# A short load ahead of the first load of a 2x2x2 average pooling

## The chip, the cores and the metric

The kernel runs on one core of one Trainium2 chip. The metric is the device time of one execution in microseconds (us), the median over several runs.

## What is computed

The input `x` is a float32 tensor of 8 x 32 x 32 x 32 x 32 (batch, channels, depth, height, width), 33.55 MB. Each output element is the mean of a block of 2 x 2 x 2 inputs, so the output is 8 x 32 x 16 x 16 x 16 float32, 4.19 MB.

```python
for i in range(out_d):
    for j in range(out_h):
        for k in range(out_w):
            window = x[:, :, 2*i:2*i+2, 2*j:2*j+2, 2*k:2*k+2]
            result[:, :, i, j, k] = np.mean(window, axis=(-3, -2, -1))
```

## The kernel before

Batch and channel together are 256 rows of 32768 floats. They are taken as two halves `t` of 128 rows, one row for each partition. Along a row the work is cut at multiples of `KF` = 256 floats. The list `plan` (L42) has eight entries: four for each half, each with 32 x 256 floats per partition, which is a tile of 128 rows with 32 KB, 4 MB in all. The first six entries are loaded by one DMA each; the last two are cut into two loads of 2 MB each. That makes ten loads, all issued from SP's queue at L77. The tiles `tin` come from a pool of five buffers (`pool_in`, L36), so the first five loads need no free buffer, and each later one waits until VectorE has finished with the buffer five tiles before.

For each loaded part, `pool_unit` (L53) runs three instructions on VectorE: an addition of neighbouring depth planes (L58), an addition of neighbouring columns (L62), and an addition of neighbouring lines with the factor 0.125 (L65), which writes into `obuf`, one buffer for each half. The result is written out by four stores (L92): one of 256 KB from ACT's queue, and on SP's queue, in this order, 2 MB (the whole first half), 1.5 MB and 256 KB.

The order of SP's queue is thus: the ten loads, then three stores. Each load or store counts up one of eight semaphores when it has landed; they are given out in turn, and a semaphore comes round again after eight transfers. A transfer that takes one up again waits until the one before on it has landed.

After tracing, `tile_avg_pool_3d_kernel` edits the program by hand. The first load, `tin` of the first entry, is moved into the opening block, ahead of SP's `Drain`, the instruction with which SP enters the barrier of all engines that opens the program:

```python
    barrier = next(
        n for n, i in enumerate(opening)
        if i.engine == load.engine and isinstance(i, mybir.InstDrain))
    program.remove(load)
    opening.insert(barrier, load)
```

So it is the first thing that SP does; the second load is issued after the barrier. The same function rewrites the end: the semaphores of the four stores (`kept`) are waited for and reset by SP's last instructions, and the others are cleared by GpSimd in ranges that leave out those of the stores.

Of the kernel before, what the change touches and what calls it, by code (L numbers as in the profile page):

```python
# [1 line left out]

# [4 lines left out]

F32 = mybir.dt.float32
KF = 256


@with_exitstack
def pool_rows(
    ctx: ExitStack,
    tc: tile.TileContext,
    x: bass.AP,
    kernel_size: int,
    out: bass.AP,
):
    nc = tc.nc  # L20
    assert kernel_size == 2, "only kernel_size == 2 supported"

    B, C, D, H, W = x.shape
    P = nc.NUM_PARTITIONS
    assert (B * C, D, H, W) == (2 * P, 32, 32, 32)
    add = mybir.AluOpType.add

    xv = x.rearrange("b c d h w -> (b c) (d h w)")  # L30
    ov = out.rearrange("b c d h w -> (b c) (d h w)")

    pool_in = ctx.enter_context(tc.tile_pool(name="pin", bufs=5))  # L36
    pool_out = ctx.enter_context(tc.tile_pool(name="pout", bufs=1))
    obuf = [pool_out.tile([P, 16 * KF], F32, name=f"obuf{t}") for t in range(2)]
    dummy = pool_out.tile([P, 1], F32, name="dummy")


    plan = [  # L42
        (0, 0, (32,)),
        (0, 32, (32,)),
        (0, 64, (32,)),
        (0, 96, (32,)),
        (1, 0, (32,)),
        (1, 32, (32,)),
        (1, 64, (16, 16)),
        (1, 96, (16, 16)),  # L50
    ]

    def pool_unit(buf, t, k0, kb):  # L53

        od = kb // 8
        a = buf.rearrange("p (o dd e) -> p o dd e", o=od, dd=2)
        b = buf[:, :od * 1024]
        nc.vector.tensor_add(  # L58
            out=b.rearrange("p (o e) -> p o e", o=od), in0=a[:, :, 0], in1=a[:, :, 1])
        bv = b.rearrange("p (e ww) -> p e ww", ww=2)  # L60
        c = buf[:, od * 1024:od * 1536]
        nc.vector.tensor_add(out=c, in0=bv[:, :, 0], in1=bv[:, :, 1])  # L62
        cv = c.rearrange("p (j hh k) -> p j hh k", hh=2, k=16)
        o0 = k0 * KF // 8
        nc.vector.tensor_tensor_reduce(  # L65
            out=obuf[t][:, o0:o0 + od * 256].rearrange("p (j k) -> p j k", k=16),
            in0=cv[:, :, 0], in1=cv[:, :, 1],
            scale=0.125, scalar=0.0, op0=add, op1=add, accum_out=dummy[:, :],
        )

    for t, k0, parts in plan:
        tin = pool_in.tile([P, 32 * KF], F32, tag="tin", name="tin")
        views = []
        o = 0
        for kb in parts:
            v = tin[:, o * KF:(o + kb) * KF]
            nc.sync.dma_start(  # L77
                out=v, in_=xv[t * P:(t + 1) * P, (k0 + o) * KF:(k0 + o + kb) * KF])
            views.append((v, k0 + o, kb))
            o += kb  # L80
        for v, k, kb in views:
            pool_unit(v, t, k, kb)

    for queue, t, k0, kb in [
        (nc.scalar, 1, 0, 2),
        (nc.sync, 0, 0, 16),
        (nc.sync, 1, 2, 12),
        (nc.sync, 1, 14, 2),  # L90
    ]:
        queue.dma_start(  # L92
            out=ov[t * P:(t + 1) * P, k0 * KF:(k0 + kb) * KF],
            in_=obuf[t][:, k0 * KF:(k0 + kb) * KF],
        )


def kernel(tc: tile.TileContext, x: bass.AP, kernel_size: int, out: bass.AP):
    nc = tc.nc
    pool_rows(tc, x, kernel_size, out)  # L100
    tc.close()
    tc.compile()  # L102
    blocks = nc.main_func.blocks

    opening, program = blocks[0].instructions, blocks[tc.starting_block_idx].instructions
    load = next(i for i in program if isinstance(i, mybir.InstDMACopy))
    assert load.engine == nc.sync.engine
    barrier = next(  # L110
        n for n, i in enumerate(opening)
        if i.engine == load.engine and isinstance(i, mybir.InstDrain))
    program.remove(load)
    opening.insert(barrier, load)

    closing = blocks[-1].instructions
    stores = [  # L120
        i for i in program
        if isinstance(i, mybir.InstDMACopy) and "out_" in i.outs[0].memref]
    kept = [u.id for i in stores for u in i.sync_info.on_update]
    kept = [n for j, n in enumerate(kept) if n not in kept[j + 1:]]
    final = next(
        i for i in closing
        if i.engine == nc.sync.engine and isinstance(i, mybir.InstDrain))
    waits = {w.id: w for w in final.sync_info.on_wait}
    closing[closing.index(final)] = mybir.InstDrain(
        name=final.name, engine=final.engine, ins=[], outs=[], is_reset_sema=False,  # L130
        sync_info=mybir.SyncInfo(
            on_wait=[w for n, w in waits.items() if n not in kept], on_update=[]))


    reset = next(
        n for n, i in enumerate(closing)
        if isinstance(i, mybir.InstDrain) and i.is_reset_sema)
    first, stop = closing[reset].reset_range_start, closing[reset].reset_range_stop
    assert isinstance(closing[reset + 1], mybir.InstISA)
    while len(closing) > reset:  # L140
        closing.pop()
    n = first
    while n < stop:
        m = n
        while m < stop and m not in kept:
            m += 1
        if m > n:
            closing.append(mybir.InstDrain(
                name=nc.get_next_instruction_name(), engine=nc.gpsimd.engine, ins=[], outs=[],
                is_reset_sema=True, reset_range_start=n, reset_range_stop=m))  # L150
            nc.gpsimd.sem_clear(range(n, m))
        n = m + 1
    for n in kept:
        w = waits[n]
        closing.append(mybir.InstEventSemaphore(
            name=nc.get_next_instruction_name(), engine=nc.sync.engine, ins=[], outs=[],
            sync_info=mybir.SyncInfo(
                on_wait=[w],
                on_update=[mybir.SyncUpdate(
                    sync_type="semaphore", id=n, ant_name=w.ant_name,  # L160
                    update_mode="sem-sub-imm", update_value=w.wait_value)])))


# [1 line left out]
_INS = ['x', 'kernel_size']  # L165
_OUTS = [((8, 32, 16, 16, 16), 'float32')]

_NUMBERS = {'kernel_size': 2}


# [26 lines left out]
```

## Time and profile before

| what | value |
|---|---|
| median of 3 runs | 91.57 us (91.52 to 91.82) |
| the profiled execution, device time | 91.76 us |
| its span, first to last instruction | 86.6 us |
| VectorE busy | 64.1 us, 74% of the span |
| mean of the DMA engines' rate over the span | 421 GB/s |
| HBM read, written | 33.55 MB, 4.19 MB |

The span ends with the last instruction that the page counts, and the last stores land after it; the device time covers them too. The DMA rows of the page give the share of the 16 DMA engines that is busy and what they moved. A packet is booked by its start and its length, so in very short windows a share can be over 1. Some packet records are missing: the page counts 36.48 MB where the kernel moves 37.75 MB. A name ending in q, as in SPq, is the engine's instruction queue: SPq at L77 is SP issuing a load, and "to landing" is the time from the issue to the completed transfer.

### The profile page before, as it was taken

To read this page: it belongs to the slowest core of one execution; us is meant where nothing else is said; L and a number is where in the kernel's file an instruction comes from. 1 tells how busy PE (TensorE), PEld (TensorE's weight loads), DVE (VectorE), ACT (ScalarE), POOL (GpSimd) and SP (SyncE) were. 2 spreads that over 40 slices of the span, in tenths; PEclk is the share of its full clock that TensorE was granted. 3 is DMA by queue.
4 is the path that set the end of the run, shared out by engine and by line. 5 is a ranking of instruction groups with operands and counts; after the bars stand their busy time and mean duration, and the time that the engine had idled before them with its cause. 6 is when DMAs were issued, how large, how long until landed. Compare 5 with 4: busy or idle time off the path is not lost.

```text
span 86.6 us, 91 instructions
## 1 busy us (share of the span) xinstructions
DVE 64.1 (74%) x40; POOL 0.2 (0%) x4
## 2 busy tenths in 40 slices
DVE  0000049993999749992999749992999999999994
POOL 0000000000000000000000000000000000000000
DMA  8889998899979999799988999699999999999999
GB/s 242 379 363 469 485 485 348 379 485 485 469 333 409 485 485 424 318 469 485 485 348 379 485 485 469 288 454 416 405 407 424 407 462 394 462 394 454 394 454 398
DMA packets 1774, 36.48 MB, mean 421 GB/s; under 512 B 192, under 2 KB 192, under 8 KB 320
## 3 DMA queue, kind: packets, MB, share of 16 engines
q1 hardware_dynamic: 1630, 36.22, 98.4%
q10 hardware_dynamic: 144, 0.26, 0.8%
HBM read 33.55 MB, written 4.19 MB: 436 GB/s over the span
## 4 chain that ended last, share of the span: by engine, by line
DMA 83%; DVE 14%; SPq 1%; issue 0%; DVEq 0%
DMA tin<-in_x_dram 83%; DVE tin L58 8%; DVE tin L62 4%; DVE obuf L65 2%; SPq L77 1%; DVE dummy L65 0%; DVEq L102 0%
## 5 line engine op out<-in xcount | busy, mean ns | idle before, releaser
L58 DVE TENSOR_TENSOR tin<-tin 128x4096 f32<-128x4096 f32 (+1 forms) x10 | 35.7, 3570 | 20.7 <-DMA tin<-in_x_dram 20.6
L62 DVE TENSOR_TENSOR tin<-tin 128x2048 f32<-128x2048 f32 (+1 forms) x10 | 18.6, 1865 | 0.3
L65 DVE CUSTOM_DVE_ANT_1 obuf<-tin 128x1024 f32<-128x1024 f32 (+1 forms) x10 | 10.1, 1011 | 0.3
L65 DVE DVE_READ_ACCUMULATOR2_ANT dummy<- 128x1 f32 x10 | 0.8, 82 | 0.0
L178 POOL MEMSET const-uint8-127<- 128x1 uint8 x1 | 0.1, 102 | 0.0
L178 POOL MEMSET const-bfloat16-1.0<- 128x1 bf16 x1 | 0.1, 101 | 0.0
L178 POOL MEMSET const-float32-0.0<- 128x1 f32 x1 | 0.1, 98 | 0.2 <-issue 0.2
L178 POOL MEMSET const-float32-1.0<- 128x1 f32 x1 | 0.1, 98 | 0.0
## 6 DMA issues: line engine op xcount, KB each, us to landing
tin<-in_x_dram SPq DMA_DIRECT2D x6, 4096.0 KB, 35.0
tin<-in_x_dram SPq DMA_DIRECT2D x4, 2048.0 KB, 38.9
out_dram<-obuf SPq DMA_DIRECT2D x1, 2048.0 KB, 36.8
out_dram<-obuf SPq DMA_DIRECT2D x1, 1536.0 KB, 8.8
out_dram<-obuf ACTq DMA_DIRECT2D x1, 256.0 KB, 9.9
out_dram<-obuf SPq DMA_DIRECT2D x1, 256.0 KB, 4.9
```

What stands on the lines that cost most here:

```text
L58: nc.vector.tensor_add(out=b.rearrange("p (o e) -> p o e", o=od), in0=a[:, :, 0], in1=a[:, :, 1])
L62: nc.vector.tensor_add(out=c, in0=bv[:, :, 0], in1=bv[:, :, 1])
L65: nc.vector.tensor_tensor_reduce(out=obuf[t][:, o0:o0 + od * 256].rearrange("p (j k) -> p j k", k=16), in0=cv[:, :, 0], in1=cv[:, :, 1], s ...
L77: nc.sync.dma_start(out=v, in_=xv[t * P:(t + 1) * P, (k0 + o) * KF:(k0 + o + kb) * KF])
L178: nc = _bacc.Bacc("TRN2", target_bir_lowering=False, num_devices=1)
```

## The change

A tile `first` of 16 partitions x 128 floats is added to the pool of output buffers, and a load of the first 512 B of 16 rows of `x` into it, 8 KB in all, is traced ahead of everything else. Nothing reads this tile. The hand edit then moves two loads instead of one ahead of SP's `Drain` in the opening block: the short one, and behind it the first load of `tin`.

```diff
     dummy = pool_out.tile([P, 1], F32, name="dummy")
+    first = pool_out.tile([16, 128], F32, name="first")
+    nc.sync.dma_start(out=first[:, :], in_=xv[:16, :128])
...
-    load = next(i for i in program if isinstance(i, mybir.InstDMACopy))
-    assert load.engine == nc.sync.engine
-    barrier = next(
-        n for n, i in enumerate(opening)
-        if i.engine == load.engine and isinstance(i, mybir.InstDrain))
-    program.remove(load)
-    opening.insert(barrier, load)
+    loads = [i for i in program if isinstance(i, mybir.InstDMACopy)][:2]
+    assert [i.outs[0].bass_ap.tensor.name.split("_")[0] for i in loads] == ["first", "tin"]
+    for load in loads:
+        assert not load.sync_info.on_wait
+        barrier = next(
+            n for n, i in enumerate(opening)
+            if i.engine == load.engine and isinstance(i, mybir.InstDrain))
+        program.remove(load)
+        opening.insert(barrier, load)
```

## The prediction

> **What bounds the kernel now.** I read the page first, its section 2 and 4: how full the DMA engines are over time, and what the chain that ended last is made of.
>
> ```profile
> DVE  0000049993999749992999749992999999999994
> ...
> DMA  8889998899979999799988999699999999999999
> ...
> DMA 83%; DVE 14%; SPq 1%; issue 0%; DVEq 0%
> ```
>
> The reader is to see that the DMA row never drops, from the second slice to the last, while VectorE (DVE) has holes up to the last third. Next come the stores, by their line in the two windows in which they are issued: is the end set by the last store's own latency, or by what lies ahead of it?
>
> ```profile
> L92 SPq DMA_DIRECT2D out_dram<-obuf x1: 348/348/348, 49.3 to 49.3; - x1
> DMA to landing us min/median/max: 9.9/23.3/36.8
> ...
> L92 SPq DMA_DIRECT2D out_dram<-obuf x2: 332/338/344, 81.1 to 85.5; - x2
> DMA to landing us min/median/max: 4.9/6.8/8.8
> ```
>
> The 2 MB store is issued at 49.3 and lands 36.8 later, at 86.1. The 1.5 MB store, issued at 81.1, lands 8.8 later, at 89.9; the last, of 256 KB, issued at 85.5, lands 4.9 later, at 90.4. So after the last load (landed by 81.2, when VectorE starts on it) the engines still have a full queue: 2 + 1.5 + 0.25 MB, 3.93 MB in 9.2 us, 427 GB/s. The loads run at the same pace: VectorE starts on the first three tiles at 12.12, 21.81 and 31.53, 9.7 us apart, 4.19 MB / 9.7 = 432 GB/s. **The kernel is one unbroken stream of transfers**, and its end is the start of that stream plus 37.75 MB of work. VectorE is done at 85.46, and the 256 KB that wait for it could come 3 us later, with about 1 us from issue to first packet (below) still inside the 4.4 us until 89.9. So a shift of the stream's start moves the end by as much, and little else does.
>
> How does the stream start? L77 in the first tenth of a us, the opening barrier's line, and the DMA share in windows of 0.1 us (the columns after the window: length, DVE and POOL busy, PEclk, share of 16 DMA engines, GB/s):
>
> ```profile
> L77 SPq DMA_DIRECT2D tin<-in_x_dram x1: 382/382/382, 0.0 to 0.0; - x1
> ...
> L178 SPq DRAIN  x1: 132/132/132, 0.4 to 0.4; - x1
> ...
> 0.90:1.00 0.10, 0.00 (x0) 0.00 (x0) 1.00 0.00 0
> 1.00:1.10 0.10, 0.00 (x0) 0.00 (x0) 1.00 6.01 1638
> 1.10:1.20 0.10, 0.00 (x0) 0.00 (x0) 1.00 4.80 1311
> 1.20:1.30 0.10, 0.00 (x0) 0.00 (x0) 1.00 2.23 655
> 1.30:1.40 0.10, 0.00 (x0) 0.00 (x0) 1.00 2.16 655
> 1.40:1.50 0.10, 0.00 (x0) 0.00 (x0) 1.00 0.00 0
> 1.50:1.60 0.10, 0.00 (x0) 0.00 (x0) 1.00 0.98 328
> 1.60:1.70 0.10, 0.00 (x0) 0.00 (x0) 1.00 0.00 0
> 1.70:1.80 0.10, 0.00 (x0) 0.00 (x0) 1.00 1.82 655
> 1.80:1.90 0.10, 0.00 (x0) 0.00 (x0) 1.00 0.00 0
> ...
> 2.80:2.90 0.10, 0.00 (x0) 0.00 (x0) 1.00 1.54 655
> ...
> 5.10:5.30 0.20, 0.00 (x0) 0.00 (x0) 1.00 0.38 164
> ```
>
> The first load is issued at 0.00 in 0.38 us. Sixteen packets of 32 KB (GB/s x 0.1 us, summed over these windows to 1.80: 524 KB) begin between 1.00 and 1.80. Their length is share x 16 x window: 18.0 x 1.6 = 28.8 engine-us, 1.80 each; the first five 6.01 x 1.6 / 5 = 1.92, the last two 1.82 x 1.6 / 2 = 1.46. Later packets take 0.38 x 16 x 0.2 = 1.22. The first packets are thus **0.58 us longer** on average than a packet in full flow. The second packets begin from 2.80 on.
>
> **What the Trainium skill says.** "DMA: Bandwidth & Descriptors", "Latency and other measured facts", gives some 600 ns to the first byte for DMAs from SP. The trace agrees: from the issue's end at 0.38 to the first packets at 1.00 is 0.62. The same page, "Why a DMA increments its semaphore by 16 and not by 1", spreads a transfer of 16 rows over 16 engines: one row of 512 B on each, so the short load stands ahead of the first load everywhere. The trace of before has no transfer of 16 rows. The same page, "Queues, rings and completion order", has descriptors of a ring taken in order, with no barrier between data descriptors. The trace fits: 9.7 us per load over 8 rows per engine is 1.21 per row across the load's end, no more than inside a load.
>
> **The change, part by part.**
>
> Added issue: one DMA on SP, ahead of the first load. The shape seems to make little difference: issues take 0.33 to 0.53 at L77, the first 0.38, the second 0.33. The first load of `tin` is handed over after two issues: 0.38 + (0.33 to 0.38) instead of 0.38. **Cost on the path: 0.33 to 0.38, taken as 0.36.** Nothing covers it, since no transfer is in flight.
>
> Added transfer: 512 B per engine, at 32 KB in 1.22 us, 0.02 us. Its own latency runs in the time in which the next issue is made; no instruction reads `first`. Taken as 0.02; bounds 0 and, if the packet holds its engine until it is complete, see rival B.
>
> The barrier: SP's Drain comes at about 0.75 instead of 0.4 and holds all engines, so the second load is issued at about 1.15 instead of 0.79, and loads 3 to 5 behind it. Cover: each engine has eight packets of the first load to do, until about 11.4; counting 1 us to the first packet, the second load could be issued 9 us later. VectorE has nothing to do before 12, ACT before its store at 59.0, and GpSimd's memsets are over by 0.43.
>
> Semaphores: the load takes the first of eight, all others move by one. By the code each store still finds itself behind the load that it was behind before (tiles 3 to 5); the seventh tile's load meets the short load's semaphore, complete some 30 us earlier: one check, 17 ns as SP's others, in a queue 30 us ahead. At the end the stores' semaphores lie at the range's end, so GpSimd may have one range to clear instead of two: that lies around 86.2 to 86.6, beside stores in flight to 90.4. Nothing; without that cover, a gain of some tenths. `first` takes 512 B per partition behind the other buffers and moves none.
>
> What the first packets lose or gain is not shown before. **Below nothing:** if the 0.58 is the cost of waking engines and memory, the short packets pay it from 1.00 on, while the second issue runs, and up to 0.58 comes back. **Above nothing:** the engines could start on the long row only when the short one is complete. I take 0: a packet that must wait for its first data has the same length behind a short one, and that need not be a matter of waking.
>
> Sum: 0.36 + 0.02 = 0.38. The profiled execution, with span 86.6, lasts 91.76, of which 1.4 follow the last landing at 90.4: 92.14 on its own terms. It lies 0.19 above the median of the runs shown, inside their spread, so the forecast is 91.57 + 0.38 = **91.95 us**, 0.4% slower. A measurement of this kernel can tell about 0.3% from no change, 0.27 us, so this lies just past the bound.
>
> **The rivals.**
>
> A, not slower: **the short load wakes the engines.** For it: early starters need 1.92 and late ones 1.46, which end at about 2.95 and 3.2, as if something common were ready only at about 1.7, whoever asked first. Against it: that is also what filling a pipeline looks like, and the wake-up can begin no earlier than now, since the first issue is still at 0.00. Price: 0.38 less what is saved. From 0.11 saved on the change is inside the 0.3%; all 0.58 saved gives 91.57 - 0.20 = 91.37, still no measurable gain. Faster by over 0.27 needs 0.65 saved, so also a part of the 0.62 from issue to first packet: with the issue shift half hidden too (0.18), 91.19.
>
> B, much slower: **the short transfer is completed first.** The skill's same page, "Anatomy of one DMA — SWDGE (gpsimd) path", prices a transfer's fixed part at some 2.0 us, mostly completion; for this queue that is an estimate. If the long row begins only then, at 2.0 instead of 1.0, the cost is 1.0: 92.57. Against it: at the ends of loads nothing of the kind shows.
>
> C: the shift is taken up along the way. The stream has dips, the lowest slice 288 GB/s, but records are missing, and no wait of the queue for a buffer empties it: four loads stand behind. Then 91.6.
>
> **How the numbers follow.** Forecast 0.55, of which 0.06 falls inside the bound; A 0.32, of which 0.15 is faster and the rest the same; B 0.07; C 0.06, the same. Faster 0.15, same 0.17 + 0.06 + 0.06 = 0.29, slower 0.49 + 0.07 = 0.56. Range: down to 91.25, inside A's faster end; up to 92.35, for the forecast with a noisy median; outside lie most of the faster cases and B, some 0.2. The forecast's own range is 91.80 to 92.10.
>
> **What would show it.** Right: `first` issued at 0.00, the first `tin` issue at 0.38; the 32 KB packets beginning at about 1.4 to 2.2, still 1.8 long; VectorE's first start at 12.12 + 0.38 = 12.5, the last store landing 0.4 later. A: VectorE starts at 12.2 or earlier, long packets of about 1.3. B: first long packets near 2.0, VectorE near 13.1. I am wrong if VectorE's first start is shifted but the time isn't (C), or the other way round.

## The result, and the profile after

The changed kernel takes 92.25 us (median of 6 runs, 92.10 to 92.26) against 91.68 (6 runs, 91.52 to 91.82) on the same chip: ratio 1.006, 95% interval 1.0046 to 1.0073, so 0.57 us slower. The forecast was 91.95, 0.38 slower than 91.57. The profiled execution lasts 92.26 us, 0.50 more than the one of before; its span is 87.0, 0.4 more.

The start of the timeline shows the cause (start, length, engine and line, what it issues or computes). First the kernel before, whose first entry on SP is five loads of `tin`, then the changed kernel:

```profile
0.00 2.66 SPq L77 DMA_DIRECT2D tin<-in_x_dram  x5
...
12.12 4.42 DVE L58 TENSOR_TENSOR tin<-tin 128x4096 f32<-128x4096 f32 x1 [12.12 <-DMA tin<-in_x_dram]
...
21.81 4.43 DVE L58 TENSOR_TENSOR tin<-tin 128x4096 f32<-128x4096 f32 x1 [1.68 <-DMA tin<-in_x_dram]
```

```profile
0.00 0.39 SPq L41 DMA_DIRECT2D first<-in_x_dram  x1
...
0.45 2.20 SPq L79 DMA_DIRECT2D tin<-in_x_dram  x4
...
12.57 4.43 DVE L60 TENSOR_TENSOR tin<-tin 128x4096 f32<-128x4096 f32 x1 [12.57 <-DMA tin<-in_x_dram]
...
22.28 4.42 DVE L60 TENSOR_TENSOR tin<-tin 128x4096 f32<-128x4096 f32 x1 [1.70 <-DMA tin<-in_x_dram]
```

The first load of `tin` is issued at 0.45 instead of 0.00. VectorE starts at 12.57 and 22.28, where before it was 12.12 and 21.81. The first three loads are later by 0.45 to 0.47, and the distance between them, 9.7 us, is the same. On the last load VectorE starts 0.58 later (81.76 against 81.18). The issue of `tin` itself and the landing of the short load, from the lines of L79 and L41 alone:

```profile
L79 SPq DMA_DIRECT2D tin<-in_x_dram x1: 415/415/415, 0.4 to 0.4; - x1
...
DMA to landing us min/median/max: 12.1/12.1/12.1
```

```profile
L41 SPq DMA_DIRECT2D first<-in_x_dram x1: 390/390/390, 0.0 to 0.0; - x1
...
DMA to landing us min/median/max: 1.7/1.7/1.7
```

`tin` lands 12.1 us after its issue in both kernels. The DMA share in short windows (column before the last; GB/s last):

```profile
1.00:1.10 0.10, 0.00 (x0) 0.00 (x0) 1.00 0.11 26
1.10:1.20 0.10, 0.00 (x0) 0.00 (x0) 1.00 0.18 46
...
1.40:1.50 0.10, 0.00 (x0) 0.00 (x0) 1.00 2.37 655
...
1.60:1.70 0.10, 0.00 (x0) 0.00 (x0) 1.00 4.57 1311
...
2.20:2.30 0.10, 0.00 (x0) 0.00 (x0) 1.00 0.78 328
```

The short packets (together 8 KB) begin at 1.0 to 1.4, and the first long ones begin at 1.40 to 2.30, 0.4 to 0.5 later than before. They begin before the short load as a whole has landed (1.7), so they don't wait for that. Whether each engine waits for its own short packet can't be read from this; a run without any short packet, below, answers it. At the end, the last two stores on SP's queue:

```profile
L94 SPq DMA_DIRECT2D out_dram<-obuf x2: 332/338/343, 81.7 to 86.1; - x2
...
DMA to landing us min/median/max: 4.8/6.7/8.6
```

The last store, issued at 86.1, lands 4.8 later at 90.9, where it was 90.4. The shift of the start has travelled through 90 us of transfers to the end.

The span is no measure for this: GpSimd has one range of semaphores to clear at its end instead of two, which takes 0.1 to 0.2 off the span and lies beside the last stores. First the line of before, then the one of the changed kernel:

```profile
L151 POOLq EVENT_SEMAPHORE_RANGE_CLEAR  x2: 44/48/53, 86.3 to 86.5; - x2
```

```profile
L156 POOLq EVENT_SEMAPHORE_RANGE_CLEAR  x1: 69/69/69, 86.9 to 86.9; - x1
```

### The profile page after: what moved, and what is told of

It is laid out like the page before. It is cut to its first block, busy times and chain, and to the rows that moved or that the text cites. A ratio compares the mean times of both kernels' runs of the same rounds, so it can differ in the third digit from the quotient of the medians.

```text
span 87.0 us, 91 instructions
## 1 busy us (share of the span) xinstructions
DVE 64.1 (74%) x40; POOL 0.2 (0%) x4
## 4 chain that ended last, share of the span: by engine, by line
DMA 82%; DVE 14%; SPq 1%; issue 0%; DVEq 0%
DMA tin<-in_x_dram 82%; DVE tin L60 8%; DVE tin L64 4%; DVE obuf L67 2%; SPq L79 1%; DVE dummy L67 0%; DVEq L104 0%
```

## The experiments

The theory to be tested, S: the cost is the time by which the first load of `tin` is issued later, and nothing else. The rivals: T, the short transfer itself holds the engines up; W, the short packets do warm the engines (their first packets get shorter), and hide a shift that would alone cost more. A hint for W was in the trace of the changed kernel: its first 16 long packets are on average 16.8 (shares of 1.40 to 2.30, summed) x 1.6 / 16 = 1.68 us long, against 1.80 before. In all that follows, the second time of each pair is the kernel before, measured beside the run.

### The short load behind the first load

```diff
-    for load in loads:
+    for load in loads[::-1]:
```

> The short load stands behind the first load of tin instead of ahead of it, both still ahead of the opening barrier. Theory S (shift): the whole cost is that the first load of tin is issued 0.45 us later; here it is issued at 0.00 again, so the time is that of before, within 0.1 us, and VectorE's first start is back at 12.1. Rival T (transfer): the short packets themselves, or their completion, hold up the 16 engines; the stream then still loses some 0.5 us, and the time is 0.5 above before. Rival W (waking: the cost would be larger than 0.57 if the short packets did not also warm the engines for the first long ones): time as before, no gain, first long packets 1.8 us long as before.

91.84 us against 91.81: ratio 1.0004 (0.9992 to 1.0015). The 8 KB are still issued ahead of the barrier, and cost nothing measurable. The second load of `tin` is as late as in the changed kernel (1.26) and the semaphores are moved by one here too, so neither has a price:

```profile
0.00 0.38 SPq L79 DMA_DIRECT2D tin<-in_x_dram  x1
...
0.43 0.42 SPq L41 DMA_DIRECT2D first<-in_x_dram  x1
...
12.11 4.43 DVE L60 TENSOR_TENSOR tin<-tin 128x4096 f32<-128x4096 f32 x1 [12.11 <-DMA tin<-in_x_dram]
```

The span falls to 86.4 here, 0.2 below before, at the same device time: that is the clearing at the end again.

### The short load from ACT's queue

```diff
-    nc.sync.dma_start(out=first[:, :], in_=xv[:16, :128])
+    nc.scalar.dma_start(out=first[:, :], in_=xv[:16, :128])
```

> The short load is issued from ACT's queue ahead of the opening barrier, so that SP's first instruction is the first load of tin again. Theory S: tin is issued at 0.00, VectorE starts at 12.1, the time is before within 0.1 us. Rival T: 0.5 us above before. Rival W: if ACT's short packets reach the engines ahead of the long ones at no cost of SP's time, the first long packets get shorter than 1.80 us and the time falls 0.1 to 0.5 below before.

91.87 against 91.81: ratio 1.0004 (0.9994 to 1.0014). A second queue takes the cost away. It says little on W: ACT issues at 0.12, so the short packets had the long ones ahead of them (landing 4.7 us after the issue).

```profile
0.00 2.46 SPq L79 DMA_DIRECT2D tin<-in_x_dram  x4
0.12 0.38 ACTq L41 DMA_DIRECT2D first<-in_x_dram  x1
```

### Two short loads

```diff
+    second = pool_out.tile([16, 128], F32, name="second")
+    nc.sync.dma_start(out=second[:, :], in_=xv[16:32, :128])
...
-    loads = [i for i in program if isinstance(i, mybir.InstDMACopy)][:2]
...
+    loads = [i for i in program if isinstance(i, mybir.InstDMACopy)][:3]
...
```

> Two short loads of 16 rows with 512 B (rows 0 to 15 and 16 to 31, into two tiles) ahead of the first load of tin on SP's queue. Theory S: each costs one start-to-start interval of SP's queue, 0.45 us, so the first load of tin is issued at about 0.90, VectorE starts first at 13.0, and the time is 0.90 to 1.1 above before (twice 0.45 to 0.57). Rival T: the same or more. Rival W (the saving is had once, from the first short load): the second one costs its full 0.45, the first 0.45 less the saving; twice the cost of one or a little more.

92.78 against 91.81: ratio 1.0104 (1.0090 to 1.0118), 0.95 us. The issues start at 0.00, 0.44 and 0.89, and VectorE follows:

```profile
0.44 0.41 SPq L43 DMA_DIRECT2D second<-in_x_dram  x1
0.89 1.68 SPq L81 DMA_DIRECT2D tin<-in_x_dram  x3
...
12.99 4.42 DVE L62 TENSOR_TENSOR tin<-tin 128x4096 f32<-128x4096 f32 x1 [12.99 <-DMA tin<-in_x_dram]
```

The price is about one start-to-start interval for each short load, and the second costs no more than the first.

### A short load of 128 rows

```diff
-    first = pool_out.tile([16, 128], F32, name="first")
-    nc.sync.dma_start(out=first[:, :], in_=xv[:16, :128])
+    first = pool_out.tile([P, 128], F32, name="first")
+    nc.sync.dma_start(out=first[:, :], in_=xv[:P, :128])
```

> The short load ahead of the first load of tin has 128 rows with 512 B instead of 16 rows, eight times the descriptors and bytes (64 KB). Theory S: only the issue counts; if it still takes about 0.39 us, the time is that of the change, 0.57 above before, plus 7 x 0.02 = 0.13 at most for the bytes. Rival T: eight packets for each engine instead of one, so the part that is the transfer's own grows eightfold: 1 us or more above before, seen as a later VectorE start with tin still issued at 0.45. Rival W: as S, or less than S if more warming helps.

92.24 against 91.81: ratio 1.0049 (1.0033 to 1.0065), 0.45 us. Eight times the rows and bytes, and the same cost: the issue takes as long as that of 16 rows, and `tin` is issued at 0.44.

```profile
L41 SPq DMA_DIRECT2D first<-in_x_dram x1: 385/385/385, 0.0 to 0.0; - x1
```

Together with the load behind `tin`, this speaks against T.

### The changed kernel again, and a delay without a transfer

> The changed kernel once more, beside the next three and the same runs of before. Theory S: 0.45 to 0.57 us above before; this is to size the cost next to the shift of tin's issue, 0.45.

92.33 against 91.85: ratio 1.0052 (1.0035 to 1.0069), 0.48 us. The two measurements of the same kernel, 0.57 and 0.48, agree within their intervals; the shift of 0.45 is inside both. The hint for W doesn't come back: the first long packets of this execution take (3.47 + 5.85 + 7.02 + 1.33 + 1.08, of which 0.01 belongs to a short packet) x 1.6 / 16 = 1.87 us. The reference scatters as well: the kernel before took 91.68 beside the first measurement, and 91.81 to 91.85 in the four later sets, so 0.57 is rather too large.

For the delay, the kernel before gets, ahead of its first load:

```diff
     opening.insert(barrier, load)
+    for _ in range(10):
+        opening.insert(barrier, mybir.InstDrain(
+            name=nc.get_next_instruction_name(), engine=nc.sync.engine, ins=[], outs=[],
+            is_reset_sema=False, sync_info=mybir.SyncInfo(on_wait=[], on_update=[])))
```

> No short load: ten Drain instructions without waits stand on SP's queue ahead of the first load of tin, a delay without any transfer. The delay d is read from the trace as the start of tin's first issue against the first thing SP does (estimated at 0.1 to 0.6 us). Theory S: VectorE's first start and the time move by d, and the long packets begin about 1.0 after tin's issue and last 1.80, as without a short load. Rival W: with a delay alone the first long packets stay at 1.80 while behind a short load they were 1.68, so a given shift costs 0.1 more here than in the changed kernel. If the span's zero moves with SP's first instruction, the comparison is made on the device time.

92.36 against 91.85: ratio 1.0060 (1.0040 to 1.0080), 0.55 us. The trace doesn't show the ten drains, and its zero is the first instruction that it does show, so the zero is another one, as these two lines tell:

```profile
0.11 0.10 POOL L182 MEMSET const-float32-0.0<- 128x1 f32 x1
...
0.40 2.12 SPq L77 DMA_DIRECT2D tin<-in_x_dram  x4
```

GpSimd's first memset begins at 0.11, not 0.23, so 0.40 is 0.52 on the other kernels' clock: delay 0.52, cost 0.55, with no transfer at all. A delay alone thus costs, within the scatter, what a short load of about the same delay costs, so no part is left to see for T. VectorE starts at 12.36, 11.96 after the issue and not 12.1. On the common clock that is 12.48, a shift of 0.36 only. The profiled execution is the fastest of its six, 92.17, and 0.41 above the profiled one of before, so it kept about the shift that its own first load shows; the 0.55 is of the six runs' median. The first long packets take (7.69 + 5.57 + 2.23 + 1.01 + 0.85) x 1.6 / 16 = 1.74 us here, with no short load to make them shorter.

### The first load behind the barrier, without and with the short load

Without: the hand edit that moves the load is left out of the kernel before.

> No short load and nothing ahead of the opening barrier: the first load of tin is issued after the barrier, as the program was traced. The barrier is then over at about 0.65, so tin is issued at about 0.7. Theory S: the time is the shift above before, 0.6 to 0.8 us. This is also the reference for the next kernel.

92.62 against 91.85: ratio 1.0079 (1.0061 to 1.0097), 0.73 us, with `tin` issued at 0.73. With: only `first` is moved.

```diff
-    loads = [i for i in program if isinstance(i, mybir.InstDMACopy)][:2]
...
+    loads = [i for i in program if isinstance(i, mybir.InstDMACopy)][:1]
...
```

> The short load stays ahead of the opening barrier, the first load of tin comes after it, at about 0.8; the short packets reach the engines at about 1.0 as in the changed kernel and the long ones some 0.8 later, which is the longest lead for waking. Theory S: only tin's issue counts; against the kernel without the short load (tin after the barrier) this is later by the difference of the two issue starts, about 0.1, though 0.39 us of issue were added: the barrier covers the rest. Rival W: the first long packets are shorter than 1.80, at best 1.22, and the time lies up to 0.5 below that of the kernel without the short load.

92.64 against 91.85: ratio 1.0082 (1.0065 to 1.0100), 0.75 us, with `tin` issued at 0.81. First the line without, then the one with the short load:

```profile
0.73 1.90 SPq L77 DMA_DIRECT2D tin<-in_x_dram  x4
```

```profile
0.81 1.85 SPq L79 DMA_DIRECT2D tin<-in_x_dram  x4
...
12.90 4.42 DVE L60 TENSOR_TENSOR tin<-tin 128x4096 f32<-128x4096 f32 x1 [12.90 <-DMA tin<-in_x_dram]
```

In the second kernel the short packets are 0.7 us ahead of the long ones, and the first long packets, from 1.70 on, are (6.14 + 4.55 + 7.08 + 0.84) x 1.6 / 16 = 1.86 us long; without the short load (7.79 + 4.51 + 3.46 + 0.98 + 0.86) x 1.6 / 16 = 1.76. The packets are not shorter behind the short load and no time is gained: W falls. (With the short load behind `tin` they take 1.85, with two short loads ahead 1.80.) And the 0.39 us of issue is nearly free here, since the barrier would have lasted almost as long.

### Two queues for the first load

The length of the first packets and their spread over 0.8 us remained unexplained. If one queue hands them out in turn, two should be faster. In these two runs there is no short load; the first load of `tin` of the kernel before is cut in two, one part from SP and one from ACT, both ahead of the barrier. First by rows:

```diff
...
-            nc.sync.dma_start(
-                out=v, in_=xv[t * P:(t + 1) * P, (k0 + o) * KF:(k0 + o + kb) * KF])
+            halves = [(nc.sync, 0, P)] if (t, k0) != (0, 0) else [(nc.sync, 0, 64), (nc.scalar, 64, P)]
+            for queue, p0, p1 in halves:
+                queue.dma_start(
+                    out=v[p0:p1], in_=xv[t * P + p0:t * P + p1, (k0 + o) * KF:(k0 + o + kb) * KF])
...
```

> The kernel before (no short load) with its first load of tin cut into two of 64 rows, one issued from SP and one from ACT, both ahead of the opening barrier. It asks whether the ramp (16 first packets that begin over 0.8 us and last 1.80) is made by one queue handing out descriptors in turn. If it is, two queues at once halve the spread, the first long packets start within 0.4 us, and the time falls 0.1 to 0.3 below before. Theory S in its narrow form (the start of tin's first issue, and nothing in the ramp, sets the time): ACT's half is issued about 0.12 later than SP's, and the time is before or up to 0.15 above.

101.19 against 91.83: ratio 1.1009 (1.0983 to 1.1034), 9.4 us. Neither of the two expectations had that. The rate row of its page (40 slices of 2.4 us):

```profile
GB/s 218 218 218 218 218 218 218 218 218 437 436 436 437 436 423 382 423 436 423 409 423 423 423 436 436 436 423 409 430 430 419 448 443 437 423 409 436 409 430 435
```

For nine slices the rate is 218 GB/s, half of the 437 that follows. The test said nothing about the ramp, so the cut was made along the row:

```diff
...
+            cuts = [(nc.sync, 0, kb)] if (t, k0) != (0, 0) else [(nc.sync, 0, 16), (nc.scalar, 16, 32)]
+            for queue, c0, c1 in cuts:
+                queue.dma_start(
+                    out=v[:, c0 * KF:c1 * KF],
+                    in_=xv[t * P:(t + 1) * P, (k0 + o + c0) * KF:(k0 + o + c1) * KF])
...
```

> The kernel before (no short load) with its first load of tin cut along the row instead: two loads of 128 rows with 16 KB, one issued from SP and one from ACT, both ahead of the opening barrier. The cut into 64 rows had left each half running at half the rate, so it said nothing about the ramp. If the ramp is made by one queue handing out its descriptors in turn, two queues shorten it and the time falls 0.1 to 0.3 below before. If the time follows the start of tin's first issue alone, it is before within 0.1 us, or up to 0.15 above.

91.75 against 91.82: ratio 0.9994 (0.9984 to 1.0003). No gain. But one line is worth reading:

```profile
13.57 4.42 DVE L58 TENSOR_TENSOR tin<-tin 128x4096 f32<-128x4096 f32 x1 [13.57 <-DMA tin<-in_x_dram]
```

VectorE starts 1.45 us later than before, and the device time doesn't move. ACT's half lands only 13.4 us after its issue; that it shares the engines with the loads behind SP's half would explain it, but wasn't tested. What sets the end of this kernel is when the transfers begin, not when the first tile is there.

## Why the prediction was right

**Direction and mechanism** were right: an unbroken stream, begun later by what stands ahead of its first issue, ends later by about as much. The kernels with all their loads at full rate line up; the cost is (ratio - 1) x the median of before in the same runs, and the drains are put on the common clock:

| kernel | first `tin` issue, us | cost, us |
|---|---|---|
| short load behind / from ACT | 0.00 | 0.04 / 0.04 |
| short load of 128 rows | 0.44 | 0.45 |
| the change, twice | 0.45, 0.44 | 0.55, 0.48 |
| ten drains | 0.52 | 0.55 |
| `tin` behind the barrier | 0.73 | 0.73 |
| the same, short load ahead | 0.81 | 0.75 |
| two short loads | 0.89 | 0.95 |

(For the change the difference of the medians is 0.57; the ratio gives 0.55.)

**The size was too small.** The measured 92.25 lies above the forecast's own range, 91.80 to 92.10, and inside the outer one, up to 92.35, only by the room that was left for a noisy median. That much was luck. Of the 0.30 between 91.95 and 92.25, 0.11 is the base: 91.57 from three runs was 91.68 from six. The other 0.19 is the cost.

**The issue term was mis-sized**: "0.33 to 0.38, taken as 0.36". I took the length of a bare issue. What counts first is the distance from one issue's start to the next's, 0.45: the issue took 0.39, just past the top of my bounds, and 0.06 passed before the next instruction. That gap was to be seen in the chain of before, where 0.05 us follow SP's 0.33 (the second load, then the gap ahead of the third):

```profile
0.79 0.33 SPq L77
1.12 0.05 issue
```

In addition the issue of `tin` took 0.415 instead of 0.382, and this counts at the start: in windows of 0.01 us the first long packet begins at 1.01 before and at 1.48 in the changed kernel, in both its profiles. In every kernel of the table it begins 0.62 to 0.64 after the end of its issue. So the term measures 0.47, which explains 0.11 of the 0.19; the remainder is inside the scatter that the repeat shows.

**The transfer term**, 0.02, is too small to be seen: eight times the bytes, and the cost is 0.45.

**The barrier and the semaphores** cost nothing, as argued: VectorE's distance between the first loads is unchanged, and with the short load behind `tin`, where both are moved as well, the time is that of before. The second load was issued at 1.27, not at the 1.15 that was forecast, still far inside its cover. One semaphore range instead of two was right too, and shows only in the span.

**Rival A** (waking) falls: the first long packets take 1.68 to 1.87 us behind a short load and 1.74 to 1.85 without one ahead, and 0.7 us of lead didn't help. **Rival B** (completion first) falls: long packets begin at 1.4, the short load landed at 1.7, and a delay without a transfer costs as much. **Rival C** falls: the shift reached the end in every run. In single executions it does so only roughly: the profiled ones, less 91.76, differ from the shift of the issue by 0.11 less to 0.17 more, and the medians of the table by about 0.1. The first reading for "what would show it" was right, VectorE at 12.57 where 12.5 was forecast; but the run with the cut along the row shows that VectorE's first start alone is no proof, and the last store's landing is the better one.

The DMA row was also read too smoothly ("never drops": it has a 6), which did no harm.

What the first packets' extra 0.58 us is made of stays open. It is not a cost that an earlier transfer pays off, and a second queue doesn't shorten the run.

## What to carry to other kernels

In a kernel that is transfers from end to end, a load ahead of the first large issue on its queue costs its start-to-start interval in full, whether it has 8 KB or 64 KB, unless something else, as the barrier here, would have held that issue anyway; behind that issue, or on another queue, the same load was free. Before paying for a warm-up, ask whether it can begin any earlier than the work itself; here it could not. Size a moved issue by the distance between starts, not by an issue's own length, and read the last landing rather than the span.

## What the runs showed of the hardware

Two loads of 64 rows with 32 KB, the halves of the first tile from two queues, moved at 218 GB/s together where 128-row loads move 437, and the kernel lost 9.4 us. It isn't the two queues: two loads of 128 rows with 16 KB cost nothing (91.75 us). A single load of 64 rows wasn't run, and why the rate is halved wasn't looked into. The Trainium skill, "DMA: Bandwidth & Descriptors", "Rules for kernel authors", advises one transfer of 128 partitions over two of disjoint halves: they share the same engines and serialize. The run agrees with the advice; what it adds to that row is the number: VectorE could start at 23.23 us instead of 12.12, so the two halves took about twice the time of the whole.

The time of SP's first issue didn't depend on the size: 0.385 us for 128 rows with 512 B, 0.390 for 16, 0.382 for 128 rows with 32 KB. The shape can matter: the two loads of 64 rows took 0.55 and 0.54. From the end of the issue of the first load of `tin` to its first packet it was 0.62 to 0.64 us in every run in which that load was whole.
